# Half of the cached keys' transposes of the last phase, from transfers to TensorE and ScalarE

## The chip, the cores and the metric

The kernel runs as one program on one core of a Trainium2 chip. The metric is the device time of an execution in microseconds (us). Three executions of the kernel before took 2345.12, 2350.16 and 2350.41 us, so their median is 2350.16 us.

A core has five engines with queues of their own: TensorE (PE in the profile; its weight loads are listed apart as PEld), VectorE (DVE), ScalarE (ACT), GpSimd (POOL) and SyncE (SP), which in this kernel issues nearly all transfers. The 16 DMA engines of the core move the data of the transfers.

## The reference, cut to what matters

One layer of a streaming encoder is computed for 2048 new frames and, with the same weights, for 8 running streams of 16 frames each, which have 512 cached positions. Each of the two token mixers (differential attention, "A", and stick-breaking attention, "B") attends over the cache and the new frames. The part around the change is the attention of the running streams:

```
def diff_attention(q, k, v, qpos, kpos, lam):
    s = jnp.einsum('bqhcd,bkhcd->bhcqk', q, k, ...) * (HEAD_DIM_A ** -0.5)
    ...
    o = jnp.einsum('bhqk,bkhe->bqhe', w, v, ...)

oa = diff_attention(qa, jnp.concatenate([cache_a_k[l], ka], axis=1),
                    jnp.concatenate([cache_a_v[l], va], axis=1), pos_s, kpos_s, lam)
ob = stick_breaking_attention(qb, jnp.concatenate([cache_b_k[l], kb], axis=1),
                              jnp.concatenate([cache_b_v[l], vb], axis=1), pos_s, kpos_s)
```

The products of queries and cached keys contract over the head dimension. The cache lies with positions along the rows, so each block of 128 positions by 128 numbers has to be transposed before TensorE can use it.

## The kernel before, in words

**Number format.** Every float32 operand of a product is scaled and split into two float16 numbers, a high and a low part (`split`, L290 for the high part on ScalarE, L295 for the low part on VectorE), and products are made from these parts.

**Stages.** A first stage (some 110 us) norms the input. A long middle stage goes through 8 units of heads (4 of A and 4 of B), each over 17 tiles of 128 rows: 16 of the new frames and one, `t == NT`, with the 128 rows of the running streams. It ends at some 1800 us. The last phase (`c2` in the code) has two kinds of work:

- For each of the 17 tiles, the gated branch outputs are read back (`inputs`, loads `hs<-o_d`, `hs<-z_d`, `wa<-g_d` and `wb<-g_d`), transposed on TensorE (`transposed`, L1162, copied out by ScalarE in L1163), multiplied with the branch weights (`branches`, L1312, 48 products of 128x512 for each tile), transposed again, multiplied with the output weights (`output`, L1341, 48 more) and normed (`normed_rows`).
- Beside these tiles runs `lane`: for each of the 8 units the attention of the running streams over the cache (`sample`). It is cut into steps, the units following one another six steps apart (`S_PERIOD`), and is spread over the first 13 tiles (`S_TILES`).

**One unit of the lane.** `cache` loads a piece of the cached keys or values (8 blocks of 128 positions, 512 KB, `dc`, three buffers). `keys(i)`, for the four pieces i = 0 to 3 in four steps that follow one another, splits a piece into `k16c` (two buffers; 16 blocks, 8 of each of the two halves of the head dimension, each of 128 positions by high and low part of 64 numbers) and has it transposed into `dks` (four buffers) by one transposing transfer from the SP queue (L754). `scores_all`, two steps behind the last of them, multiplies all four pieces with the queries (L764 to L766 for the new frames, L772 for the cache) into PSUM banks of the tag "s" and makes the weights, which a transposing transfer turns (`dwt`, L580). `values(i)` and `output_cached(i)` use them (L803, copied out by ScalarE in L806), and `finish` adds the new frames' part.

**PSUM.** There are three banks of the tag "s". In the last phase they hold the results of `transposed`, those of `scores_all`, and those of `finish`. A fourth user has to wait until one of them is read out.

**What sets the order.** The source interleaves the two kinds of work by hand (`interleave`, by cost). Each engine's final order is not that of the source: a planner that works when the program is built (`schedule_with_timeline_sim=True`) puts an instruction on its engine where its own estimate of time has the operands ready. On the chip each engine then keeps that order, and waits where an operand is later than planned. All transfers of this phase are issued by SP, in order: one that waits for its operand holds up those behind it.

Of the kernel before, what the change touches and what calls it, by code (L numbers as in the profile page):

```python
# [17 lines left out]
F16 = mybir.dt.float16  # L18
# [7 lines left out]
P = 128  # L26
# [83 lines left out]
def layer_kernel(ctx: ExitStack, tc: tile.TileContext, a: dict):  # L110
    nc = tc.nc
    V, S, G, T = nc.vector, nc.scalar, nc.gpsimd, nc.tensor
# [74 lines left out]
    def bank(tag, dt=F32):  # L187
        return ps.tile([P, 512 if dt == F32 else 1024], dt, tag=tag, name=f"ps_{tag}", bufs=BANKS[tag])
# [5 lines left out]
    id16 = con.tile([P, P], F16, name="id16")  # L194
# [92 lines left out]
    def split(hi, lo, src, s, on=None):  # L287

        if on is S:
            S.activation(out=hi, in_=src, func=AF.Identity, scale=s)  # L290
        elif on is G:
            G.tensor_scalar(out=hi, in0=src, scalar1=s, scalar2=0.0, op0=ALU.mult, op1=ALU.add)
        else:
            V.tensor_scalar(out=hi, in0=src, scalar1=s, scalar2=None, op0=ALU.mult)
        V.scalar_tensor_tensor(out=lo, in0=src, scalar=s, in1=hi, op0=ALU.mult, op1=ALU.subtract)  # L295
# [426 lines left out]
    def sample(U, dec, qpad, cs):  # L722
# [26 lines left out]
        def keys(i):  # L749
            kc = box.pop((nk, i))  # L750
            k16 = dec.tile([P, 16, 2, 64], F16, tag="k16c", name="k16c", bufs=2)
            split(k16[:, :, 0, :], k16[:, :, 1, :], kc.rearrange("p j (c d) -> p (j c) d", c=2), sk, S)
            box["k", i] = kt = dec.tile([P, 8, 2, P], F16, tag="dks", name="dks", bufs=4)
            nc.sync.dma_start_transpose(out=kt.rearrange("p j c n -> p (j c) n"), in_=k16.rearrange("p j f d -> p (j f d)"))  # L754

        def scores_all():

# [68 lines left out]
        for i in range(4):  # L826
            steps[1 + i] += [one(keys, i)]
            steps[8 + i] += [one(output_cached, i)]
# [83 lines left out]
    with tc.tile_pool(name="p0", bufs=1) as p0:  # L912
# [34 lines left out]
        pt = bank("t")  # L947
# [33 lines left out]
        pt = bank("t")  # L981
# [442 lines left out]
```

## Time and profile before

| what | before |
|---|---|
| median of three runs | 2350.16 us |
| profiled execution, device time | 2352.01 us |
| its span | 2350.2 us |
| PE busy | 2124.9 us, 90% of the span |
| DVE, ACT busy | 1725.1 us and 1644.4 us |
| mean granted TensorE clock | 0.965 |
| first and last transposing transfer of cached keys | 1828.9 us and 2169.9 us |

How to read it: busy times are sums over one profiled execution. The list of waits puts each idle stretch of an engine down to the work that ended it, "who waited" to the left of the arrow and "for what" to the right. In a line of groups or of the order in time, `L754` is line 754 of the kernel, `out<-in` are the program's names, and `xN` is a count. A row of a table of stretches gives the busy us of each engine in that stretch, then the granted TensorE clock, the busy share of the DMA engines and GB/s. The stretch that matters is the one from 1850 to 2200 us, in which most of the lane lies.

### The profile page before, as it was taken

The page shows a single profiled execution, that of the slowest core. Times are in us where ns is not written, and L with a number is a line of the kernel's source. Part 1 is how long each engine was busy: PE and PEld are TensorE (multiplying, and loading weights), DVE is VectorE, ACT ScalarE, POOL GpSimd, SP SyncE. Part 2 cuts the span into 40 slices and gives each one's busy share as a digit, 9 for nine tenths or more (in the row PEclk, how much of TensorE's full clock was granted, in tenths as well). Part 3 has the DMA queues.
Part 4 walks back from the last instruction along what each step waited for, and adds up shares of the span by engine and source line. Part 5 has one row for each costly group of instructions (what it writes and reads, how often), then busy time and mean ns, then how long its engine had stood idle before and what let it go on. Part 6 is the DMA issues. An engine that isn't in the chain of part 4 may idle for free. (4 is left out here: it accounts for less than half of the span.)

```text
span 2350.2 us, 42700 instructions
## 1 busy us (share of the span) xinstructions
PE 2124.9 (90%) x15272; PEld 1144.5 (49%) x15272; DVE 1725.1 (73%) x3652; ACT 1644.4 (70%) x3260; POOL 705.0 (30%) x610
## 2 busy tenths in 40 slices
PE   5898899998999999899999979998996879988998
PEld 3554454444555445445545545554553344544443
DVE  4848866779875667978667797877688877777663
ACT  4557878787886778878677777866777656665541
POOL 1533012446300334731033474103335111221111
PEclk8999899999999999999999999999996989999999
DMA  9766759887895988867577787766687999999531
GB/s 334 252 203 177 165 127 263 180 188 163 207 227 131 213 199 189 175 175 191 139 188 175 186 171 185 192 146 149 142 175 162 288 238 250 237 249 243 157 103 48
DMA packets 834357, 445.34 MB, mean 189 GB/s; under 512 B 537210, under 2 KB 777130, under 8 KB 833632
## 3 DMA queue, kind: packets, MB, share of 16 engines
q1 hardware_dynamic: 833196, 442.24, 76.5%
q8 instruction: 119, 1.95, 0.3%
q14 instruction: 94, 0.77, 0.1%
q10 hardware_dynamic: 948, 0.39, 0.1%
HBM read 245.60 MB, written 69.24 MB: 134 GB/s over the span
## 5 line engine op out<-in xcount | busy, mean ns | idle before, releaser
L622 POOL TENSOR_TENSOR sc_p<-sc_p,sc_n 128x127 f32<-128x127 f32 (+7 forms) x192 | 314.2, 1640 | 834.8 <-DVE sc_n L616 812.5
L428 PE MATMUL ps_mm<-wb,hs 128*128 128x512 f16 x1632 | 412.1, 380 | 5.1 <-DMA hs<-hT_d 3.0
L428 PEld LDWEIGHTS <-hs 128*128 128x128 f16 x3120 | 275.8, 99 | 264.5 <-issue 14.8
L428 PE MATMUL ps_mm<-wa,hs 128*128 128x512 f16 x1488 | 377.7, 384 | 9.0 <-DVE qbuf L463 3.8
L616 DVE TENSOR_TENSOR_SCAN sc_n<-ps_s,sc_n,zero_t 128x512 f32<-128x512 f32 x192 | 245.5, 1279 | 80.8 <-ACT ps_s L119 77.5
L639 PE MATMUL ps_s<-k,qst 128*128 128x512 f16 (+3 forms) x640 | 227.5, 356 | 37.2 <-DVE sc_n L616 25.8
L573 DVE TENSOR_TENSOR sc_n<-sc_p,sc_n 128x128 f16<-128x128 f32 (+7 forms) x192 | 211.5, 1106 | 51.8 <-ACT sc_n L572 51.3
L504 PEld LDWEIGHTS <-hs 128*128 128x128 f16 x1632 | 155.6, 98 | 181.4 <-DVE qst L532 5.5
L119 ACT ACTIVATE sc_p<-ps_s,usc 128x512 f32<-128x512 f32 (+3 forms) x320 | 204.3, 638 | 35.3 <-PE ps_s L640 27.9
L640 PE MATMUL ps_s<-k,qst 128*128 128x512 f16 (+3 forms) x640 | 227.1, 356 | 0.0
L572 ACT CAST sc_n<-sc_p 128x128 f16<-128x128 f32 (+7 forms) x192 | 154.9, 811 | 78.9 <-POOL sc_p L622 76.0
L700 PE MATMUL ps_o<-v,wt 128*128 128x128 f16 x1088 | 172.2, 226 | 35.1 <-DMA wt<-sc_n 35.1
L119 ACT ACTIVATE ps_s<-ps_s,usc 128x512 f32<-128x512 f32 (+3 forms) x328 | 199.4, 608 | 0.0
L504 PE MATMUL ps_t<-wb,hs 128*128 128x512 f16 x816 | 192.9, 380 | 2.5 <-DVE qst L532 2.2
L504 PE MATMUL ps_t<-wa,hs 128*128 128x512 f16 x816 | 192.3, 381 | 3.1 <-DVE qst L532 2.2
L1341 PE MATMUL ps_o<-wo,wb 128*128 128x512 f16 x816 | 189.2, 386 | 4.0 <-ACT wb L1163 4.0
L701 PE MATMUL ps_o<-v,wt 128*128 128x64 f16 x1088 | 158.3, 198 | 0.0
L700 PEld LDWEIGHTS <-wt 128*128 128x128 f16 x1088 | 105.6, 101 | 100.1 <-DMA wt<-sc_n 46.4
L558 DVE TENSOR_SCALAR_CACHE_REDUCE sc_n<-ps_s,usc 128x512 f32<-128x512 f32 (+3 forms) x160 | 106.5, 666 | 42.2 <-PE ps_s L640 22.9
L616 DVE TENSOR_TENSOR_SCAN sc_n<-ps_s,zero_t 128x128 f32<-128x128 f32 (+3 forms) x128 | 104.2, 815 | 41.0 <-ACT ps_s L119 38.0
L558 DVE TENSOR_SCALAR_CACHE_REDUCE sc_p<-ps_s,usc 128x512 f32<-128x512 f32 (+3 forms) x160 | 106.4, 665 | 35.6 <-PE ps_s L640 26.1
L701 PEld LDWEIGHTS <-wt 128*128 128x128 f16 x1088 | 103.4, 101 | 54.5 <-issue 1.9
(358 smaller groups left out, 4531.3 us busy)
## 6 DMA issues: line engine op xcount, KB each, us to landing
hs<-hT_d SPq DMA_DIRECT2D x130, 512.0 KB, 4.4
g_d<-gt SPq DMA_DIRECT2D x68, 256.0 KB, 4.4
wb<-g_d SPq DMA_DIRECT2D x26, 512.0 KB, 5.7
out_dram<-pr SPq DMA_DIRECT2D x204, 64.0 KB, 2.4
o_d<-o SPq DMA_DIRECT2D x136, 64.0 KB, 2.0
hs<-o_d SPq DMA_DIRECT2D x17, 512.0 KB, 5.1
out_dram<-x SPq DMA_DIRECT2D x17, 512.0 KB, 2.8
wide<-in_w_ada_dram SPq DMA_DIRECT2D x8, 1024.0 KB, 7.8
```

The source lines that it names most:

```text
L119: i = S.activation(**kw)
L428: T.matmul(box["p"], box["h"][:, hi, k, :], U["w"][k][:, wi, :], start=(n == 0), stop=(n == 3 * KT - 1))
L504: T.matmul(box["g"][:, 0:gw], box["h"][:, hi, k, :], U["wg"][k // per][:, k % per, wi, :], start=(j == 0), stop=(j == 3 * KT - 1))
L558: V.tensor_scalar(out=dst[:, lo : lo + n], in0=p[:, 0:n], scalar1=sc_pos, scalar2=None, op0=ALU.mult, op1=ALU.max, accum_out=job["mx"][:, ...
L573: V.tensor_tensor(out=lo, in0=src, in1=hi, op=ALU.subtract)
L616: V.tensor_tensor_scan(out=dst[:, lo : lo + n][:, ::-1], data0=src[:, 0:n][:, ::-1], data1=zero_t[:, 0:1].to_broadcast([P, n]), initial=fi ...
L622: G.tensor_tensor(out=p[:, 0:m], in0=p[:, 0:m], in1=n[:, 1 : m + 1], op=ALU.mult)
L639: T.matmul(p[:, 0:n], qst[:, c, :], kk[:, c, 0:n], start=True, stop=False)
L640: T.matmul(p[:, 0:n], qst[:, 2 + c, :], kk[:, c, 0:n], start=False, stop=not diag)
L700: T.matmul(po[:, c * P : (c + 1) * P], wt[:, wj, :], vt[:, c, :, :], start=first, stop=False)
L701: T.matmul(po[:, c * P : c * P + 64], wt[:, nb + wj, :], vt[:, c, 0, :], start=False, stop=last)
L1341: T.matmul(po, st["y"][:, yi * 8 + k, :], wo[j * 4 + k // 2][:, wi, k % 2, :], start=(n == 0), stop=(n == 3 * KT - 1))
```

## The change

In `keys`, the pieces with even i (0 and 2) are transposed by a transfer as before. For those with odd i (1 and 3), the transfer is gone. In its place, for each half of the 16 blocks, a bank of the tag "s" is taken, TensorE transposes 8 blocks of 128x128 float16 into it, and ScalarE copies the bank's 128x1024 float16 into the half of `dks` that it belongs to. Over the 8 units that is 16 of the 32 transfers of L754, 256 transposes on TensorE and 32 copies on ScalarE. Loads, splits, buffers and all products are as before, and so is what is computed.

```
             box["k", i] = kt = dec.tile([P, 8, 2, P], F16, tag="dks", name="dks", bufs=4)
-            nc.sync.dma_start_transpose(out=kt.rearrange("p j c n -> p (j c) n"), in_=k16.rearrange("p j f d -> p (j f d)"))
+            kv = kt.rearrange("p j c n -> p (j c) n")
+            if i % 2 == 0:
+                nc.sync.dma_start_transpose(out=kv, in_=k16.rearrange("p j f d -> p (j f d)"))
+                return
+
+            for half in range(2):
+                pt = bank("s", F16)
+                for j in range(8):
+                    T.transpose(pt[:, j * P : (j + 1) * P], k16[:, half * 8 + j, :, :].rearrange("p f d -> p (f d)"), id16)
+                S.copy(out=kv[:, half * 8 : half * 8 + 8, :], in_=pt.rearrange("p (j n) -> p j n", n=P))
```

## The prediction

> **What bounds the kernel now.** I read the table of stretches first, because a share over the whole span says nothing about the one stretch that the change touches. Its columns are the stretch, its length, busy us of PE, PEld, DVE, ACT and POOL, the granted clock, the DMA share and GB/s.
>
> ```profile
> 1850.00:2200.00 350.00, 305.88 (x2629) 157.66 (x2629) 264.21 (x554) 224.74 (x320) 66.18 (x41) 0.96 0.95 245
> 1900.00:1950.00 50.00, 39.26 (x362) 20.49 (x361) 36.85 (x79) 31.69 (x47) 6.44 (x5) 0.86 1.00 241
> 2210.00:2340.00 130.00, 126.64 (x806) 62.50 (x803) 66.66 (x154) 45.88 (x63) 18.68 (x14) 0.99 0.24 80
> ```
>
> From 1850 to 2200 us, where the cached attention runs beside the tiles, PE is busy 305.9 of 350 us and idle 44.1, and the DMA engines are busy 95%. After the cached attention (2210 to 2340) PE is idle only 3.4 of 130 us at a DMA share of 24%. So PE sets the end, through its work plus 44 us of idle time, and that idle time comes with full DMA engines. Next, what ended PE's idle time (1850 to 2210 us: total, times, longest):
>
> ```profile
> PE ps_t L803 <- ACT ot L806: 11.2, 6, 3.0
> PE ps_t L803 <- DMA dwt<-dsc: 7.3, 7, 2.9
> PE ps_s L1162 <- ACT wb L1163: 5.5, 3, 3.4
> PE ps_s L1162 <- DVE dsc L616: 5.5, 2, 3.2
> PE ps_o L1341 <- ACT wb L1163: 3.3, 1, 3.3
> PE ps_s L772 <- DMA dks<-k16c: 3.2, 2, 1.7
> PE ps_s L1162 <- DVE dsc L558: 2.7, 1, 2.7
> PE ps_t L815 <- ACT ot L806: 2.4, 2, 2.0
> ```
>
> Only 3.2 us of it names the transfers that are to be halved. Most names ScalarE or VectorE, so I looked at what these wait for, and at the SP queue, in the same stretch:
>
> ```profile
> ACT k16c L290 <- DMA dc<-in_cache_b_k_dram: 29.8, 10, 6.9
> ACT wb L119 <- DMA wb<-g_d: 23.7, 8, 7.0
> ACT k16c L290 <- DMA dc<-in_cache_a_k_dram: 23.3, 7, 5.2
> ...
> SPq L754 <- DVE k16c L295: 34.8, 13, 4.8
> ```
>
> ScalarE stands 53.1 us (17 times, 3.1 us each) in front of cached keys that haven't landed. One such case in order of time:
>
> ```profile
> 1908.68 1.15 ACT L290 ACTIVATE k16c<-dc,s_c 128x1024 f16<-128x1024 f32 x1 [3.66 <-DMA dc<-in_cache_a_k_dram]
> 1909.86 1.29 DVE L295 SCALAR_TENSOR_TENSOR k16c<-dc,s_c,k16c 128x1024 f16<-128x1024 f32 x1 [2.86 <-ACT k16c L290]
> ...
> 1912.94 1.28 DVE L616 TENSOR_TENSOR_SCAN dsc<-ps_s,dsc,zero_t 128x512 f32<-128x512 f32 x1 [1.32 <-ACT ps_s L119]
> ...
> 1914.28 1.98 PE L1162 MATMUL ps_s<-id,wa 128*128 128x128 f16 x16 [3.21 <-DVE dsc L616]
> ```
>
> A late load of keys holds ScalarE, then VectorE, then a bank "s" that PE needs: 3.2 us of PE. Late loads are thus behind much of the 44 us, by way of engines with time to spare (ACT is busy 224.7 of 350).
>
> **The change, part by part.**
>
> *Removed: 16 of 32 transposing transfers.*
>
> ```profile
> L754 SPq DMA_TRANSPOSE dks<-k16c x32: 1512/3282/6898, 1828.9 to 2169.9; - x32
> DMA to landing us min/median/max: 4.3/5.1/9.4
> ...
> dks<-k16c SPq DMA_TRANSPOSE x29, 5.1
> ```
>
> One holds the SP queue for 3.28 us in the middle (1.5 at least) and lands after 5.1; 29 of the 32 start between 1850 and 2210 us (last row). Sixteen take 16 x 3.28 = 52 us off that queue. I estimate that they take about as much off the DMA engines, 52 of 0.95 x 350 = 333 us, which would lower their share to about 0.80; the bounds are 24 us (16 x 1.51) and 82 us (16 x 5.1). SP also no longer waits in front of those sixteen for VectorE's `k16c` (34.8 us for all that the view names so), so the loads of `dc`, `g_d` and `o_d` behind them go out earlier. What this is worth to PE lies between nothing (the loads wait for one of three `dc` buffers instead) and everything that late transfers explain: the rows named above with ACT `ot` (11.2 and 2.4), `dwt` (7.3), `dks` (3.2) and `wb` for L1341 (3.3), 27.4 us. I take two thirds, 18 us: half of the transposes stay in the queue, but the DMA engines leave saturation.
>
> *Added on PE: 256 transposes.* The same operation with the same shape stands in the chain of waits, between other matmuls:
>
> ```profile
> 2271.94 8.85 PE ps_o L1341 x41
> 2280.79 0.89 PE ps_s L1162 x16
> 2281.68 5.18 PE ps_mm L1312 x24
> ```
>
> Sixteen take 0.89 us of PE's time, 55.6 ns each, weight loads hidden. 256 x 55.6 ns = 14.2 us. Nothing is taken off PE, so this lies on the path whole, unless it falls into idle time (that gain is counted in the waits).
>
> The Trainium skill, "TensorE: Matmul & The Clock Gate", Part 4 (PE-mode transpose), gives about 275 ns for such a transpose inside a kernel and says that transposes don't count as PE activity for the clock. Taken one behind the other, that would be 70 us instead of 14.2. The row above and the clock of 0.99 in a stretch with L1162 in it don't agree; the row is used.
>
> *Added on PE: a wait of its own.* The transposes need the low part of `k16c`, written a moment before, while the transfer that needed it stood on SP. The planner puts them where it expects that part, and PE waits if it is late. Behind them on PE stand the tiles' products (L1312, L1341), and for those wait VectorE and with it the outputs. That PE's order follows the planner is seen here, where products of the lane and of the tile alternate:
>
> ```profile
> 1843.84 0.39 PE L772 MATMUL ps_s<-dks,qpad 128*32 128x512 f16 x2
> ...
> 1844.17 1.04 PE L1341 MATMUL ps_o<-wo,wb 128*128 128x512 f16 x4
> ...
> 1845.13 0.39 PE L772 MATMUL ps_s<-dks,qpad 128*32 128x512 f16 x2
> ```
>
> The lower bound is 0 (PE gets there later than the keys). The upper is that half of ScalarE's 17 waits of 3.1 us fall on odd pieces and reach PE in full: 8.5 x 3.1 = 26 us. The nearest row is an operand that comes to PE by a chain ending in a transfer, `dwt`: 7.3 us over 12 transfers, 0.6 each. 16 x 0.6 = 9.7 us; I take that, as ScalarE and PE are tied to each other many times in a tile and rarely far apart.
>
> *Added: 32 users of the three banks "s".* The last phase has 100 such uses (four for each of 17 tiles, four for each of 8 units), and PE's waits for a bank come to 5.5 + 5.5 + 2.7 us in the rows above, about 0.14 each. 32 more at that price: 4.4 us. Bounds 0 and twice that.
>
> *Added on ACT: 32 copies.*
>
> ```profile
> L1163 ACT COPY wb<-ps_s x46: 988/1008/1078, 1867.6 to 2327.5; 128x1024 f16<-128x1024 f16 x46
> ```
>
> 32 x 1.01 = 32.3 us. ACT has 125 us idle in the stretch and the copies go there, so I cost them at nothing; `scores_all` needs the last piece only two steps later. If that cover were gone, what stands behind a copy (L806, L1163, the next split) would be late by up to 1.0 us and PE with it: at most 32 us.
>
> *Sum against the profiled execution (2352.0 us, of which 2350.2 are span).* 14.2 + 9.7 + 4.4 - 18 = +10.3, so 2362.3. The profiled time is 1.9 us above the median of the runs, so the forecast is about 2361 us for the median.
>
> **The rivals.**
>
> *Faster: the DMA engines were the bound.* If the whole 27.4 us of late-transfer waits go and PE never waits for the split, the sum is 14.2 - 27.4 = -13.2, or 2337 us. For it: a DMA share of 0.95 in the stretch, and PE nearly without idle time once it is 0.24. Against it: only 3.2 us name `dks`, and loads still come through one queue with half the transposes. It decides from the point where relief passes the 28 us of new costs. The Trainium skill speaks for this side: "Vector Engine: DVE Perf Modes", Rules for kernel authors, would give a 128x128 transpose to TensorE where a result in PSUM is fine. By rows, a piece costs 0.89 us of PE and two copies of 1.01 us there, and 3.28 us of the SP queue by transfer.
>
> *No change.* The relief just pays for the transposes and the new waits are half as large: 14.2 + 7 - 21 = 0, 2350 us. The three terms would have to meet by chance; the planner's new order could do it.
>
> *Much slower: PE is exposed to late keys.* The loads stay as late (they are held by buffers, not by the queue), and PE waits for the split as often as ScalarE does for the load: 14.2 + 26 + 4.4 - 13.7 (half of 27.4) = +31, 2381 us. For it: 17 of the 29 pieces in the stretch were late. Against it: with fewer transposes the loads land earlier.
>
> *The clock falls.* In 1900 to 1950 us it is 0.86, against 0.96 in the whole stretch. If transposes, or the waits in front of them, held it there, the products would take 305.9 x (0.96/0.86 - 1) = 36 us more: about 2397 us. Against it stands the 0.99 after 2210 us with transposes in every tile.
>
> **How the numbers follow.** Chances: the forecast 0.44, faster 0.28, no change 0.12, much slower 0.12, clock 0.04. The forecast's own range is 2350 to 2375 us. Ends for 8 in 10: 2335 us, which takes in the faster case, and 2384 us, which takes in the exposed one; the clock case and the far sides are left out. 0.3% of the time is 7 us, about what a measurement of this kernel can tell from no change. Faster by more than that: 0.28 (nearly all of the faster rival and a little of the others). Within: 0.18 (the third rival, the forecast's low end). Slower: 0.54.
>
> **What would show each step right or wrong.** (1) The transposes of `k16c` on PE: x256 at some 219 ns in the list and about 0.9 us for 16 in the order of time. (2) PE's waits for `k16c`: near 10 us if the forecast holds, near 26 if PE is exposed, near 0 if it isn't. (3) DMA share from 1850 to 2200 us: near 0.80. (4) ScalarE's waits for `dc`: well below 53 us, or the relief has failed. (5) PE's idle time in the stretch: about 40 us; 20 or fewer means the faster rival. The prediction is wrong at its root if loads aren't late because of the queue and the transposes at all, or if the planner's new order moves waits about by more than these terms.

## The result, and the profile after

The changed kernel takes 2358.38 us in the median (five runs, 2355.52 to 2361.89), the kernel before 2350.16 us (five runs, 2345.12 to 2350.81). The ratio is 1.0042 with a 95% interval of 1.0025 to 1.0059: 6 to 14 us slower. The profiled execution has a span of 2353.7 us, against 2350.2 before, so the two profiles differ by less than half of what the timed runs do. Part of that is where the last phase begins. Its first transposes on TensorE start at 1813.8 us before and at 1813.0 us after, and in the profiles of the experiments anywhere from 1811 to 1821 us, though no edit touches the stages ahead of them. Before:

```profile
1813.81 1.04 PE L1162 MATMUL ps_s<-id,hs 128*128 128x128 f16 x8
```

After:

```profile
1812.97 1.04 PE L1171 MATMUL ps_s<-id,hs 128*128 128x128 f16 x8
```

From there to the end of the span the last phase takes 536.4 us before and 540.7 us after, 4.3 us more. This length is given for the other profiles too, as it leaves out the scatter of the earlier stages. Terms read from one profile each are good to a few us and no better.

First the table of stretches of the changed kernel, with the stretch of the prediction, and then that of the whole last phase from 1826 us (where the first cached keys are split in these two profiles) to the end. Columns as before: length, busy us of PE, PEld, DVE, ACT, POOL, clock, DMA share, GB/s.

```profile
1850.00:2200.00 350.00, 313.86 (x2846) 169.20 (x2839) 261.21 (x550) 249.72 (x349) 59.07 (x40) 0.95 0.80 219
...
1826.00:2353.70 527.70, 469.91 (x3878) 247.90 (x3876) 360.38 (x767) 322.55 (x443) 87.35 (x60) 0.95 0.66 183
```

The same last phase of the kernel before:

```profile
1826.00:2350.20 524.20, 459.46 (x3623) 233.09 (x3622) 362.40 (x769) 293.20 (x411) 92.15 (x60) 0.96 0.77 200
```

From 1826 us to the end TensorE was busy 459.5 and idle 64.7 us before, and is busy 469.9 and idle 57.8 us after: 10.4 us more work, 6.9 us less idle time, together the 3.5 us by which the spans differ. Counted from the first transposes instead, it is 11.3 us more work and the same 6.9 us less idle time. So the change did both things that it could: it gave TensorE work and took idle time from it, and the first is larger. The DMA share from 1850 to 2200 us fell from 0.95 to 0.80, ScalarE got 25 us busier.

What ended TensorE's idle time in the changed kernel, 1850 to 2210 us (total, times, longest; L762 are the new transposes, L763 their copies, and the lines behind them have moved by nine: L1171 is the L1162 of before, L812 the L803):

```profile
PE ps_t L812 <- DMA dwt<-dsc: 8.4, 5, 2.9
PE ps_t L812 <- ACT ot L815: 5.7, 3, 2.7
PE ps_s L762 <- DVE k16c L295: 4.8, 2, 3.8
PE ps_s L762 <- ACT wa L1172: 4.0, 1, 4.0
PE ps_s L773 <- ACT wb L1172: 3.0, 1, 3.0
PE ps_s L1171 <- ACT dks L763: 2.7, 3, 1.2
PE ps_s L1171 <- ACT wb L1172: 2.3, 2, 1.6
...
PE ps_t L824 <- ACT ot L815: 0.8, 1, 0.8
```

The waits for `ot` went from 13.6 to 6.5 us, and that for `dks` by transfer is gone. New are those of the transposes for the split (4.8) and for a bank (4.0), and of the tiles' transposes for a bank that a copy of keys holds (2.7). The waits of ScalarE and of the SP queue in the same stretch show where the earlier stalls went. ScalarE, changed kernel:

```profile
ACT k16c L290 <- DMA dc<-in_cache_b_k_dram: 19.5, 7, 5.4
ACT k16c L290 <- DMA dc<-in_cache_a_k_dram: 10.6, 6, 4.2
```

and SP:

```profile
SPq L747 <- DVE v16c L295: 39.2, 17, 6.8
SPq L747 <- DVE k16c L295: 22.9, 10, 3.3
...
SPq L756 <- DVE k16c L295: 6.5, 5, 3.4
```

Before, the largest row of this kind for the loads `dc` was:

```profile
SPq L747 <- DVE v16c L295: 10.6, 7, 3.3
```

ScalarE waits 30.1 us for cached keys, 53.1 before. SP waits only 6.5 us in front of the remaining transposes for a split, but 62 us in front of the loads `dc` until the splits have given back one of the three buffers (14.2 us before, 3.6 of it for `k16c`). The loads are now held by their buffers and less by the queue.

The new transposes themselves, as the list of everything that touches `k16c` has them (duration in ns: least, middle, most), and the first two batches in order of time:

```profile
L762 PE MATMUL ps_s<-id,k16c x256: 216/219/314, 1830.9 to 2175.3; 128*128 128x128 f16 x128
...
L756 SPq DMA_TRANSPOSE dks<-k16c x16: 1577/3444/8447, 1828.4 to 2162.9; - x16
...
PE ps_s L762: 7.3, 4
```

```profile
1829.57 1.28 DVE L295 SCALAR_TENSOR_TENSOR k16c<-dc,s_c,k16c 128x1024 f16<-128x1024 f32 x1 [0.47 <-ACT k16c L290]
...
1830.91 1.07 PE L762 MATMUL ps_s<-id,k16c 128*128 128x128 f16 x16 [1.69 <-DVE k16c L295]
1831.57 1.93 ACT L763 COPY dks<-ps_s 128x1024 f16<-128x1024 f16 x2 [1.00 <-PE ps_s L762]
...
1842.45 1.07 PE L762 MATMUL ps_s<-id,k16c 128*128 128x128 f16 x16 [0.85 <-DVE k16c L295]
1843.59 0.99 ACT L763 COPY dks<-ps_s 128x1024 f16<-128x1024 f16 x1
...
1846.70 0.99 ACT L763 COPY dks<-ps_s 128x1024 f16<-128x1024 f16 x1
```

Sixteen take 1.07 us, and the last of them alone 0.22, so they start (1.07 - 0.22)/15 = 57 ns apart, which was the price in the prediction (55.6). The second batch shows what a copy in ScalarE's queue does: its second bank is full at 1843.5 and read out at 1847.7.

### The profile page after: what moved, and what is told of

It is laid out like the page before. It is cut to its first block, busy times and chain, and to the rows that moved or that the text cites. A ratio compares the mean times of both kernels' runs of the same rounds, so it can differ in the third digit from the quotient of the medians.

```text
span 2353.7 us, 43235 instructions
## 1 busy us (share of the span) xinstructions
PE 2128.8 (90%) x15528; PEld 1155.8 (49%) x15528; DVE 1724.7 (73%) x3652; ACT 1673.6 (71%) x3292; POOL 700.3 (30%) x610
```

## The experiments

All were timed in five rounds, in four groups, each beside the kernel before on the same chip; its medians there were 2354.01, 2353.18, 2353.61 and 2349.16 us, so ratios are compared and not times. 0.1% is 2.4 us.

**The costs without the relief.** All four pieces go by transfer; the odd ones are transposed and copied out as well.

```
             nc.sync.dma_start_transpose(out=kt..., in_=k16...)
+            for half in range(2 * (i % 2)):
+                pt = bank("s", F16)
+                for j in range(8):
+                    T.transpose(pt[:, j * P : (j + 1) * P], k16[:, half * 8 + j, :, :]..., id16)
+                junk = tiny.tile([P, 1024], F16, tag="junk", name="junk", bufs=1)
+                S.copy(out=junk, in_=pt)
```

> All four pieces of keys go by transfer as in the kernel before; the two odd ones are transposed by TensorE and copied out by ScalarE as well, into a scratch tile that nobody reads. So this has the costs of the change without its relief. Theory (the change costs TensorE 14 us of work and some 5 to 14 us of waits, and gets part of it back from fewer transfers): 20 to 28 us over before, 2370 to 2378 us. Rival (the transposes fall into idle time of TensorE, and the loss comes from a new order of the planner): at most 8 us over before, 2358 us or less.

Measured: 2371.26 us, ratio 1.0076 (1.0061 to 1.0092), 14 to 22 us over before, 18 in the middle. The middle is just under the theory's 20 to 28, and the whole interval is clear of the rival's 8. The last phase of its profile:

```profile
1826.00:2363.20 537.20, 475.40 (x3888) 251.56 (x3886) 359.42 (x771) 323.57 (x444) 85.49 (x60) 0.95 0.75 196
```

Busy is up by 15.9 us, and idle time (61.8) has not grown at all. Counted from the first transposes, busy is up by 14.4 us, and the last phase takes 547.9 us, 11.5 more than before, in what is the fastest of the six executions (2365.0 us). So work is most of the cost; the waits that come with it are about 18 - 14 = 4 us, and anything from 0 to 8 us by the interval.

**The relief without the costs.** The odd pieces are not turned, and the products read the even one in their place.

```
             split(k16[:, :, 0, :], k16[:, :, 1, :], ..., sk, S)
+            if i % 2:
+                box["k", i] = box["k", i - 1]
+                return
```

> The odd pieces of keys are loaded but neither split nor transposed; the products use the even piece before them in their place, so the scores of half of the cached positions come from other keys. So the sixteen transfers are gone without anything in their place, and sixteen splits (one instruction of ScalarE and one of VectorE each) go with them. Theory (late transfers are behind part of TensorE's idle time): 10 to 20 us below before, 2330 to 2340 us. Rival (loads are late because of their buffers, not because of the transposes): within 5 us of before.

The expectation has one mistake: the edit stands behind the split, so all 32 splits were made, and what is gone are the sixteen transfers alone. Measured: 2340.72 us, ratio 0.9952 (0.9938 to 0.9967), 8 to 15 us below before, 11 in the middle. The rival (within 5 us) falls. Its profile:

```profile
1826.00:2339.50 513.50, 462.54 (x3635) 237.32 (x3634) 357.45 (x780) 297.09 (x416) 89.99 (x60) 0.94 0.69 191
1850.00:2200.00 350.00, 316.98 (x2730) 165.49 (x2728) 266.09 (x573) 234.14 (x334) 66.92 (x43) 0.93 0.84 228
```

Idle time of TensorE is 51.0 us, 13.7 less than before, and the last phase, counted from its first transposes, takes 522.2 us, 14.2 less. Costs and relief together, 18 - 11 = 7 us, are within the 6 to 14 us of the change.

**What the relief consists of.** Two runs keep one half each of what a transfer does. In the first, SP still waits for the split, but moves little:

```
+            if i % 2:
+                box["k", i] = box["k", i - 1]
+                few = dec.tile([P, 2, 64], F16, tag="few", name="few", bufs=1)
+                load(out=few, in_=k16[:, 15, :, :])
+                return
```

> As the relief alone (odd pieces split but not turned, the products use the even piece before them), but a small transfer of 128x128 float16 that reads the split odd piece is put on the SP queue in place of the transposing one. So SP still waits for the split, in order, and hardly anything is moved. Theory A (transposes cost time by what they occupy of the DMA engines): as the relief alone, 2336 to 2346 us. Theory B (they cost time because SP waits for the split in front of later loads): back to before, 2350 to 2357 us.

In the second the transfer stays, with a source that is always ready:

```
+            if i % 2:
+                box["k", i] = box["k", i - 1]
+                nc.sync.dma_start_transpose(out=kt..., in_=wo[0])
+                return
```

> As the relief alone (the products use the even piece in place of the odd one), but the transposing transfer of an odd piece stays and takes output weights that lie ready as its source, into a tile that nobody reads. So the DMA engines and the queue have as many transposes as before, but sixteen of them wait for nothing. Theory A (occupied DMA engines): as before, 2350 to 2357 us. Theory B (SP waiting for the split): as the relief alone, 2336 to 2346 us.

Measured: 2335.57 us, ratio 0.9931 (0.9913 to 0.9948), and 2336.78 us, 0.9932 (0.9912 to 0.9953). Both are 16 us below before in the middle (11 to 21), so neither has less than the whole relief and neither theory holds alone. Their last phases take 518.4 and 522.0 us. The idle time of TensorE in them is 53.4 and 54.8 us, 10 to 11 us less than before, so in idle time the relief of all three runs is 10 to 14 us. What these two are faster beyond that is busy time, 6.7 and 4.5 us less than before for the same 3695 matmuls. It goes with the granted clock: counted from the first transposes to the end it is 0.96 in both, 0.95 before and 0.94 in the relief alone. That the edits raised the clock isn't shown. The load-only run in the stretch from 1850 to 2200 us:

```profile
1850.00:2200.00 350.00, 312.88 (x2733) 163.41 (x2732) 269.42 (x579) 235.48 (x334) 69.90 (x44) 0.97 0.99 253
```

The DMA engines are busy 99%, more than before, and TensorE is idle 37.1 us in place of 44.1, with a last phase 14.4 us shorter. A full set of DMA engines is not what bounds this phase.

These runs and the relief have one thing in common that the change has not: the scores no longer need the odd pieces, the last one among them. So that alone was tried, with all 32 transfers in place.

```
-    T.matmul(pc[...], qpad[...], box["k", i][:, b * 4 : b * 4 + 4, c, :], ...)
+    T.matmul(pc[...], qpad[...], box["k", i - i % 2][:, b * 4 : b * 4 + 4, c, :], ...)
```

> The kernel before with all 32 transposing transfers of keys, but the products read the even piece in place of the odd one after it (so the scores of half of the cached positions come from other keys, as in the relief alone). Nothing is taken off the queue or the DMA engines. Theory C (what the relief, wait-only and load-only runs had in common is that the scores no longer hang on the last piece, and that is their gain): 2334 to 2342 us, as those. Theory A+B (a transfer that SP waits for and that also occupies the DMA engines is what costs; taking away either is enough): as before, 2349 to 2357 us.

Measured: 2351.99 us, ratio 0.9991 (0.9979 to 1.0002). Its stretch from 1850 to 2200 us:

```profile
1850.00:2200.00 350.00, 309.39 (x2661) 161.16 (x2660) 264.95 (x560) 228.09 (x322) 64.06 (x41) 0.96 1.00 249
```

Theory C falls: the dependence is worth nothing that can be measured while the transfers are there. At a DMA share of 1.00 this run has no gain, and at 0.99 the load-only run has the whole of it, so the share doesn't decide. What is left of the theories is that a transposing transfer costs time when SP both waits for its operand and then spends long on it, and that taking away either is enough. This is reached by exclusion and not shown. The wait-only run keeps only a part of the waits: SP's idle stretches in front of its sixteen small transfers come to 24 us, and those in front of the sixteen transposes that stay to 71 us (127 us for all 32 before). Also, each edit gives the planner another order. The three runs with a gain share one thing more: the `k16c` buffer of an odd piece comes free sooner. Against that as the cause, no idle stretch of ScalarE before is put down to such a buffer. Why the two halves don't add up isn't settled by these runs.

**Is the loss proportional to the pieces?** Three runs change how many and which pieces go to TensorE, each by the one condition.

All four pieces on TensorE:

```
-            if i % 2 == 0:
+            if i < 0:
```

The even pieces in place of the odd ones:

```
-            if i % 2 == 0:
+            if i % 2:
```

The last piece alone:

```
-            if i % 2 == 0:
+            if i < 3:
```

> All four pieces are transposed by TensorE, none of the keys by transfer. Theory (work and waits grow with the number of pieces, the relief less so once the transfers have left saturation): another 14 us of work and 5 of waits for less than 10 us of relief, 14 to 26 us over before, 2364 to 2376 us. Rival (transfers still bind with half of the transposes left): below the changed kernel, under 2355 us.

> As the changed kernel with the pieces exchanged: the even pieces are transposed by TensorE, the odd ones by transfer. Theory (the cost is work and waits that every piece brings): as the changed kernel, 6 to 14 us over before, 2358 to 2368 us. Rival (the cost hangs on where the planner happened to put the transposes): outside of that, below 2354 or above 2372 us.

> Only the last of the four pieces (8 of 32) is transposed by TensorE. Theory C (the way from the last piece's load to the scores is what is worth shortening): half of the cost of the change (7 us of work, about 2 of waits) for all of its gain, 2344 to 2352 us. Theory A+B: half of the cost and half of the relief, 2354 to 2358 us.

| pieces on TensorE | ratio to before | interval |
|---|---|---|
| 1 and 3 (the change) | 1.0042 | 1.0025 to 1.0059 |
| 0 and 2 | 1.0003 | 0.9991 to 1.0014 |
| 3 | 1.0024 | 1.0010 to 1.0037 |
| all four | 1.0009 | 0.9998 to 1.0020 |

All four (2353.77 us) cost less than the change's two, and the other two (2354.35 us) cost nothing that can be told from before, at the edge of what that run's rival said. The theory had 14 to 26 us over before for all four, and the measured loss is at most 5, as that run's rival said (below the changed kernel); it had 6 to 14 us for the even pieces, and it is at most 3. Only the last piece alone (2359.12 us, 2 to 9 us over before) is about half of the change, near what theory A+B had for it, and over theory C's range. The loss is thus not a price per piece. The profile with all four shows that more idle time can be had for more work:

```profile
1826.00:2352.00 526.00, 480.57 (x4137) 261.92 (x4134) 357.90 (x769) 350.50 (x476) 86.46 (x60) 0.97 0.56 168
```

TensorE is busy 21.1 us more than before and idle 45.4 us, 19.3 less. There SP has no transposing transfer of keys left. Part of this result may be the clock: in the eleven runs with all four the granted clock of the whole run is 0.967 to 0.971, 0.968 in the mean, and 0.965 in the mean of the runs before. If all of the 2125 us that TensorE is busy go with the clock, that difference of 0.3% is worth some 7 us, as an estimate; no run tells it from the relief. Why the even pieces are better than the odd ones, by the same count of instructions, isn't settled. The two profiles don't help much: the one of the even pieces is the slowest of its twelve runs and that of the change the fastest of its five (spans of 2356.6 and 2353.7 us). By their last phases (538.3 and 540.7 us) the even pieces are 2.4 us better, which one profile each can't tell from scatter. That the planner's order makes the difference fits, but isn't shown.

**Fewer waits on TensorE?** The transposes and copies of the odd pieces one step of the lane later than the split:

```
+            box["k16", i] = k16
+
+        def keys_turned(i):
             ...
             steps[1 + i] += [one(keys, i)]
+            if i % 2:
+                steps[2 + i] += [one(keys_turned, i)]
```

> As the changed kernel, but the transposes and copies of an odd piece are put one step of the lane later than its split. Theory (TensorE's waits for a fresh split, 4.8 us in the profile of after, and those for a bank behind it are part of the cost): 3 to 8 us below the changed kernel, 2350 to 2355 us. Rival (the loss is the work of TensorE alone): as the changed kernel, 2356 to 2361 us.

Measured: 2361.40 us, ratio 1.0031 (1.0018 to 1.0044), which can't be told from the change, as the rival said. TensorE's wait for the split fell to 3.3 us (from 7.3), but another took its place:

```profile
PE ps_t L817 <- DMA dwt<-dsc: 20.7, 7, 8.3
PE ps_s L767 <- DVE k16c L295: 3.3, 2, 3.1
```

**Other ways out of the costs.** With all four pieces on TensorE, VectorE copied out every first bank (`(V.tensor_copy, S.copy)[half](out=..., in_=...)`), and in another run the attention weights were transposed by TensorE, too:

```
+        if job["t"] == NT:
+            for f in range(2):
+                pt = bank("s", F16)
+                for j in range(nb):
+                    T.transpose(pt[:, j * P : (j + 1) * P], w16[:, (f * nb + j) * P : (f * nb + j + 1) * P], id16)
+                S.copy(out=seg["wt"][:, f * nb : f * nb + nb, :], in_=pt[:, 0 : nb * P]...)
+            return
         nc.sync.dma_start_transpose(out=seg["wt"][:, 0 : 2 * nb, :], in_=w16[:, 0 : 2 * nk])
```

> All four pieces by TensorE, with the first bank of each piece copied out by VectorE and the second by ScalarE, instead of both by ScalarE. In the profile with all keys on TensorE, its transposes and those of the tiles wait 11 us for banks that ScalarE reads out. Theory (a bank given back sooner saves part of that): 3 to 8 us below all keys on TensorE, 2346 to 2351 us, which would be below before. Rival (VectorE's own queue is as late): as all keys on TensorE, 2352 to 2358 us.

> All four pieces of keys by TensorE, and the attention weights of the running streams too (12 transfers of 10 blocks become 120 transposes and 24 copies of 128x640). In the profile with all keys on TensorE the largest wait of TensorE is for these weights, 12.5 us. Theory (a late transfer costs more than 6.7 us of work on TensorE): 2 to 8 us below all keys on TensorE, 2345 to 2352 us. Rival (the three banks are the limit by now, and each further user waits): at or over all keys on TensorE, 2354 us or more.

Measured: 2363.57 us, ratio 1.0042 (1.0026 to 1.0059), and 2371.48 us, 1.0076 (1.0059 to 1.0092); all four pieces alone had 1.0009. Both are worse, the first beyond the range of its rival too. In the first, TensorE's waits name the new reader (1826 to 2330 us):

```profile
PE ps_s L1171 <- DVE dks L763: 7.4, 3, 4.0
```

With all four pieces copied out by ScalarE the same wait was:

```profile
PE ps_s L1171 <- ACT dks L763: 6.9, 6, 3.2
```

So the banks came free no sooner for TensorE, and the theory falls. The 0.5 us more doesn't explain the loss, though. In the profiles its last phase (540.4 us) is only 2.3 us longer than with all four copied by ScalarE, and begins 6.9 us later. The granted clock of its six runs is lower throughout (0.959 to 0.966, against 0.967 to 0.971). What made it slower isn't shown.

In the second, TensorE waits for weights that were written just before (L584 are their transposes):

```profile
PE ps_s L584 <- ACT dsc L572: 14.5, 4, 6.6
PE ps_s L584 <- ACT dsc L290: 4.9, 1, 4.9
...
PE ps_s L584 <- DVE dsc L573: 2.7, 5, 0.7
```

That is 22.1 us in these three rows, where with all four pieces it waited 12.5 us for the same weights by transfer:

```profile
PE ps_t L812 <- DMA dwt<-dsc: 12.5, 9, 2.8
```

The work added here besides, 120 transposes, is another 6.7 us by the price of 55.6 ns. Here the exposure of which the prediction was afraid for the keys did happen.

**The gain without the change?** Since transfers whose source lies ready were nearly free, all four transfers were put one step of the lane later than their splits, with TensorE left alone:

```
+            box["k16", i] = k16
+
+        def keys_turned(i):
+            k16 = box.pop(("k16", i))
             ...
             steps[1 + i] += [one(keys, i)]
+            steps[2 + i] += [one(keys_turned, i)]
```

> The kernel before, all four pieces by transfer, with each transposing transfer put one step of the lane later than its split, so that SP meets loads first that it used to hold up. Theory (SP waiting for a split in front of later loads is half of what a transposing transfer costs, and the gain of the load-only run can be had without changing the result): 3 to 15 us below before, 2338 to 2350 us. Rival (the planner's order leaves SP waiting all the same, or the later keys cost what the earlier loads gain): within 3 us of before or over it.

Measured: 2349.89 us, ratio 0.9998 (0.9986 to 1.0009). No gain, as the rival said. SP (1826 to 2210 us; L759 is the transposing transfer here) still waits in front of the transfers, and also for the buffers of the loads:

```profile
SPq L747 <- DVE v16c L295: 22.7, 9, 6.9
SPq L759 <- PE ps_s L1168: 21.5, 8, 6.4
SPq L747 <- DVE k16c L295: 14.1, 6, 3.7
```

No version that computes the whole result was faster than the kernel before.

## Why the prediction was right, and where only its sum was

The forecast was 2361 us by a sum of +10.3 us. The timed difference is 8.2 us by the medians and 9.9 by the ratio.

*Work, 14.2 us.* Held. The spacing of 57 ns agrees with the 55.6 of the row it was taken from, and TensorE was busy 11.3 us more in the change and 14.4 us more with the costs alone, counted from the first transposes of the last phase. The granted clock stayed at 0.95 in the stretch (0.96 before), and over whole runs it was 0.964 to 0.972 (0.965 in the profile before), so the clock rival is gone. The 275 ns that the Trainium skill ("TensorE: Matmul & The Clock Gate", Part 4: PE-mode transpose) gives for a transpose inside a kernel isn't the price here. The trace has 219 ns for the duration of one, and 57 ns of TensorE's time.

*Own wait, 9.7 us.* The profile has 7.3 us, in four of the sixteen batches. That is the right size for a wait, between the two bounds, and PE was not exposed in full. How much of it is time lost is another matter, as the next term shows.

*Banks, 4.4 us.* Not visible as a sum: waits for a bank "s" that copies of keys hold are 3.0 us, those of the new transposes for a bank 4.0, but the older ones, 13.7 us in the prediction's rows, fell by more than that. What can be said is that both waits together, put at 14.1 us, came to some 4 us of time (0 to 8) when the relief was left out (18 less 14.2).

*Copies on ScalarE, nothing.* Not contradicted: 32 copies made it 29 us busier, its waits for keys fell by 23, and the 4 us of the costs alone leave little room for them. No run has the copies by themselves.

*Relief, 18 us.* Too much by the run that leaves the sixteen transfers out: 11 us (8 to 15). By time the two that keep a half of what they do are 16 us faster (11 to 21), but the idle time that went, which is what the term stands for, is 10 to 14 us in all three. What the profile was to show was right in direction and partly in size (share 0.80 as estimated, waits for `dc` down from 53.1 to 30.1 us, idle time in the stretch 36.1 against about 40). The reason given, that the DMA engines leave saturation, was wrong: at a share of 0.99 the load-only run had all of the relief, and at 1.00 the run without the dependence had none.

So two terms were mis-sized, the waits by some 10 us too much and the relief by some 7, and the errors nearly cancelled. The kind of the result, more cost than relief, was foreseen for the right reason on the side of the cost. That the sum came so near is luck. The faster rival ("the DMA engines were the bound") fell with the time itself, and its premise fell with the load-only run. That the planner's order can move waits about by as much as these terms, which the prediction named as a way to be wrong, may be what the pieces 0 and 2 show: the same work without a loss. So the loss of this change is explained by its costs and its relief, but it doesn't belong to the operation alone.

## What to carry to other kernels

Work that is put on the engine which sets the end has to be counted at its full time first: here 14 us of work cost 18. What it takes from elsewhere comes back only as far as that engine was idle because of it, here 11 us. A resource at 95% beside a bound engine isn't by that the cause of its idle time: fill it to 99% with work that nobody waits for, and see whether the time moves. Where a planner orders the instructions, measure a few equivalent placements before a loss or gain of 0.4% is put down to an operation.

## What the runs showed of the hardware that was not expected

VectorE reads a bank of 128x1024 float16 out in 680 ns where ScalarE takes 999, as the list of what touches `dks` has it for the run that shares the copies (ns: least, middle, most):

```profile
L763 ACT COPY dks<-ps_s x32: 990/999/1022, 1838.4 to 2188.4; 128x1024 f16<-128x1024 f16 x32
L763 DVE COPY dks<-ps_s x32: 675/680/693, 1840.3 to 2184.8; 128x1024 f16<-128x1024 f16 x32
```

and that run was slower than the one with all copies on ScalarE all the same. Sixteen transposing transfers of 128x2048 float16 whose source lies ready cost nothing that could be measured: 0.9932 of before with them (0.9912 to 0.9953), 0.9952 without (0.9938 to 0.9967).
